# The first SwiGLU products of layers 0 and 1 in two matmuls a block instead of three

## The chip, the cores and the metric

One core of a Trainium2 chip runs the whole program. The time is device microseconds of one execution. The text names the engines as the profile does: PE multiplies, PEld loads its weights, DVE is the vector engine, ACT the scalar engine, POOL the GpSimd engine, SP issues transfers.

## What is computed

Four residual layers on 256 tokens of 1024 channels. Each layer has a token mixer (short gated convolution in layers 0 and 3, neighbourhood attention in layer 1, a long convolution in layer 2) and then a SwiGLU channel mixer. Ahead of each stands an RMS norm, and each adds to the residual. The change concerns the SwiGLU:

```python
def swiglu(h, w13, w2):                       # h: 256 x 1024, normed
    g, u = jnp.split(h @ w13, 2, axis=-1)     # w13: 1024 x 5632
    return (jax.nn.silu(g) * u) @ w2          # w2: 2816 x 1024
```

Layer 1's window attention and layer 2's filters of length 512 do not change. The filters depend on no input token, so the kernel makes them early.

## The kernel before, in words

**Numbers in two parts.** All large products take float32 operands as a rounded part and a remainder, both in float32r: a weight tile `w` becomes `hi` and `lo`, an activation `x` becomes `xh` and `xl`. A product is `hi·xh + hi·xl + lo·xh`. A *block* here is one 128x128 weight tile against 256 tokens, so a block is three products of 256 columns.

**Two forms of a block.** `mm3` (L122) issues three matmuls of 256 columns into one half of a PSUM bank. `mm2` (L129) issues two. `xh` and `xl` lie beside each other in one tile, so the first streams both as 512 columns past `hi` and fills a whole bank (the left half `hi·xh`, the right half `hi·xl`). The second adds `lo·xh`, 256 columns, to the left half. The two halves must be added afterwards. `join` (L136) does this: ACT copies the right half out of PSUM, DVE adds it to the left half.

**The SwiGLU** is `ffn` (L292). The first product has 44 weight columns a layer (22 for g, 22 for u), each of 8 blocks, so 352 blocks. The second has 8 output tiles of 22 blocks each. `HALVES` (L49) says which layers use the two-matmul form in the first product: layers 2 and 3. They run `product2` (L313), which takes one hidden tile `j` (128 channels) at a time: columns g and u of `j`, two whole banks, and then `gated2` (L296). Layers 0 and 1 run the loop at L352: two hidden tiles at a time in the halves of two banks (four columns), and then `gated` (L334). In the trace `pg` and `pu` are the banks of g and u, `R` is the norm's factor, `hid` the result in two parts, which the second product (bank `po`) reads. The second product uses `mm2` in all four layers, so its block `k` needs the two parts of hidden tile `k`.

**Weights.** `wload` (L99) brings each weight column of 512 KB by a transfer on SP's queue (tile `st`, 5 buffers), ACT rounds it to `hi` (L109, 6 buffers) and DVE or POOL subtracts to make `lo` (6 buffers). `POOL_FILTERS` (L48) gives POOL 17% of the `lo` subtractions in layers 0 and 1. In layers 2 and 3 DVE does them all.

**Filters.** While layers 0 and 1 run their SwiGLU, `fill(j)` (L881) adds one step of the filter work of layer 2 after every second pair of hidden tiles (slots of `FILTER_SLOTS`, L41): either a step of 8 PE matmuls (`ff`) with elementwise work on DVE, ACT and POOL, or a step of 14 PE matmuls (`fl`, `fh`) with a reciprocal, two products and two sums on DVE. `product2` calls `fill(j // 2)` after odd `j`, so the number of slots is the same in both forms.

**Order.** Each engine runs its instructions in the order in which they stand in its own stream. A scheduler sets that order when the program is built. `Pipeline` (L269) only says which step of the loop issues which work. PSUM has 8 banks for everything.

Of the kernel before, what the change touches and what calls it, by code (L numbers as in the profile page):

```python
# [45 lines left out]
AHEAD = 6  # L46

POOL_FILTERS = 0.17  # L48
HALVES = (2, 3)  # L49
LOW_DMA_FROM = 5  # L50


# [1 line left out]
def encoder(ctx: ExitStack, tc: tile.TileContext, A: dict, out: bass.AP):  # L54
# [13 lines left out]
    def bank(name):  # L68
        return pp.tile([P, 512], F32, tag="ps", name=name)
# [222 lines left out]
    def ffn(layer, norm, nxt, fill):  # L292
        with tc.tile_pool(name=f"ffn{layer}", bufs=NP_, side="right") as hp:
# [19 lines left out]
            def product2(line):  # L313
                parts = []
                for j in range(FT):
                    ps = [bank(f"pg{layer}_{j}"), bank(f"pu{layer}_{j}")]
                    for i in range(2):
                        w = wload(A["f_w13"][layer, i * FT + j], D, f"w13_{layer}_{i * FT + j}")
                        if j < 2:
                            parts.append((ps[i], w))  # L320
                            if len(parts) == 4:
                                in_group2(parts, norm)
                        else:
                            in_tile2(ps[i], w, norm)
                        line.tick()
                    if j == 1:
                        line.add(line.now + NORM_LAG, norm.stats)
                        line.add(line.now + NORM_LAG + 1, gated2, 0, before)
                        line.add(line.now + NORM_LAG + 1, gated2, 1, ps)
                    elif j:  # L330
                        line.add(line.now, gated2, j, ps)
                    before = ps
# [16 lines left out]
            line = Pipeline()  # L349
            if layer in HALVES:  # L350
                product2(line)
            for j in range(0 if layer in HALVES else NP_):  # L352
                pg, pu = bank(f"pg{layer}_{j}"), bank(f"pu{layer}_{j}")
# [652 lines left out]
```

## Time and profile before

| what | value |
|---|---|
| three runs | 1216.48, 1219.21, 1221.54 us, median 1219.21 |
| the profiled execution | 1219.07 us, span 1217.3 us |
| mean granted PE clock | 0.997 |
| PE busy | 1194.1 us, 98% of the span |
| weight loads (PEld) | 1105.2 us, 91% |
| DVE busy | 948.5 us, 78% |
| ACT busy | 681.9 us, 56% |
| POOL busy | 180.1 us, 15% |

The span runs from the first profiled instruction to the last. 1.8 us of the profiled execution's time lie outside it. Matmuls are pipelined, so a matmul's own duration is longer than the step to the next one. The pace of PE is read from the starts of matmuls. DVE and ACT start an instruction slightly before the one ahead has ended, so their busy time in a window is a little less than the sum of durations.

### The profile page before, as it was taken

What the parts mean: (1) busy time and instruction counts of PE and PEld (TensorE: products, weight loads), DVE (VectorE), ACT (ScalarE), POOL (GpSimd) and SP (SyncE); (2) the same over time, 40 slices, a digit from 0 to 9 for tenths busy, and PEclk for the clock granted to TensorE, in tenths of its full rate; (3) what the DMA queues carried; (4) which work ended last, traced back from release to release, by engine and by line L of the source; (5) the groups of instructions that cost most, each with busy time, mean ns of one, the idle gap of its engine ahead of it and who ended that gap; (6) DMA issues with size and microseconds to landing.
All of it is one profiled execution on the core that took longest, in us unless ns stands there. A gap on an engine that the chain in (4) does not pass through costs nothing.

```text
span 1217.3 us, 21366 instructions
## 1 busy us (share of the span) xinstructions
PE 1194.1 (98%) x8242; PEld 1105.2 (91%) x8242; DVE 948.5 (78%) x1421; ACT 681.9 (56%) x1096; POOL 180.1 (15%) x175
## 2 busy tenths in 40 slices
PE   7999999999998999999999999999999999999998
PEld 5899999988998999999898999888888889888887
DVE  6987877988676678788948996887765888787753
ACT  5655554555567665455547775665554555665531
POOL 0001121331454122232322120000000000000000
PEclk9999999999999999999998999999999999999999
DMA  9754656566666555666689996655565554655661
GB/s 309 233 191 135 215 176 206 171 209 210 218 182 189 164 187 175 198 193 179 208 255 268 296 282 211 208 191 190 175 190 190 194 191 162 210 183 187 175 203 39
DMA packets 72095, 241.82 MB, mean 199 GB/s; under 512 B 10231, under 2 KB 11641, under 8 KB 71865
## 3 DMA queue, kind: packets, MB, share of 16 engines
q1 hardware_dynamic: 61408, 211.68, 54.1%
q0 software_dynamic: 8256, 22.84, 8.1%
q10 hardware_dynamic: 2328, 5.93, 1.3%
q8 instruction: 65, 1.06, 0.4%
q14 instruction: 38, 0.30, 0.1%
HBM read 234.10 MB, written 6.29 MB: 197 GB/s over the span
## 4 chain that ended last, share of the span: by engine, by line
PE 91%; DMA 3%; DVE 2%; POOL 2%; ACT 1%; issue 1%; SPq 0%; POOLq 0%; ACTq 0%; DVEq 0%
PE po L133 14%; PE ai L133 7%; PE po L134 7%; PE pu L133 7%; PE pg L133 7%; PE ai L134 4%; PE pu L125 3%; PE pg L125 3%; PE pu L126 3%; PE pg L127 3%; PE pu L127 3%; PE pg L126 3%; PE pu L134 3%; PE pg L134 3%; PE ci L127 2%; PE ci L125 2%
## 5 line engine op out<-in xcount | busy, mean ns | idle before, releaser
L109 ACT CAST hiw<-stw 128x1024 fp32r<-128x1024 f32 (+1 forms) x276 | 280.3, 1024 | 245.0 <-PE po L133 67.0
L78 DVE TENSOR_TENSOR low<-stw,hiw 128x1024 fp32r<-128x1024 f32 (+1 forms) x254 | 305.6, 1208 | 121.2 <-ACT hiw L109 119.7
L133 PE MATMUL po<-hid,hiw 128*128 128x512 f32 x704 | 248.3, 396 | 0.0
L134 PE MATMUL po<-hid,low 128*128 128x256 f32 x704 | 197.8, 281 | 0.0
L133 PEld LDWEIGHTS po<-hid,hiw 128*128 128x128 f32 x704 | 132.1, 188 | 31.9 <-DVE hid L78 0.5
L133 PE MATMUL ai<-xsm,hiai 128*128 128x512 f32 x376 | 133.7, 398 | 0.0
L134 PEld LDWEIGHTS po<-hid,low 128*128 128x128 f32 x704 | 132.6, 188 | 0.0
L133 PE MATMUL pg<-xsf,hiw 128*128 128x512 f32 x352 | 126.8, 396 | 0.0
L133 PE MATMUL pu<-xsf,hiw 128*128 128x512 f32 x352 | 126.5, 395 | 0.0
L134 PE MATMUL ai<-xsm,loai 128*128 128x256 f32 x376 | 106.0, 282 | 0.0
L125 PE MATMUL pu<-xsf,hiw 128*128 128x256 f32 x352 | 99.3, 282 | 0.0
L125 PE MATMUL pg<-xsf,hiw 128*128 128x256 f32 x352 | 99.0, 281 | 0.0
L126 PE MATMUL pu<-xsf,hiw 128*128 128x256 f32 x352 | 98.9, 281 | 0.0
L127 PE MATMUL pg<-xsf,low 128*128 128x256 f32 x352 | 98.9, 281 | 0.0
L134 PE MATMUL pg<-xsf,low 128*128 128x256 f32 x352 | 98.9, 281 | 0.0
L127 PE MATMUL pu<-xsf,low 128*128 128x256 f32 x352 | 98.9, 281 | 0.0
L126 PE MATMUL pg<-xsf,hiw 128*128 128x256 f32 x352 | 98.9, 281 | 0.0
L134 PE MATMUL pu<-xsf,low 128*128 128x256 f32 x352 | 98.8, 281 | 0.0
L78 POOL TENSOR_TENSOR low<-stw,hiw 128x1024 fp32r<-128x1024 f32 (+1 forms) x22 | 53.9, 2452 | 223.7 <-ACT hiw L109 193.1
L133 PEld LDWEIGHTS ai<-xsm,hiai 128*128 128x128 f32 x376 | 71.0, 189 | 17.1
L133 PEld LDWEIGHTS pu<-xsf,hiw 128*128 128x128 f32 x352 | 66.1, 188 | 15.7
L133 PEld LDWEIGHTS pg<-xsf,hiw 128*128 128x128 f32 x352 | 66.1, 188 | 15.4
(238 smaller groups left out, 3035.7 us busy)
## 6 DMA issues: line engine op xcount, KB each, us to landing
stw<-in_f_w SPq DMA_DIRECT2D x208, 512.0 KB, 3.4
stw<-in_f_w SPq DMA_DIRECT2D x64, 448.0 KB, 3.4
stai<-in_a_w_in SPq DMA_DIRECT2D x45, 512.0 KB, 3.7
stbi<-in_b_w_qkv SPq DMA_DIRECT2D x24, 512.0 KB, 4.2
stci<-in_c_w_in SPq DMA_DIRECT2D x24, 512.0 KB, 9.2
loci<-in_c_w_in POOLq DMA_DIRECT2D x19, 512.0 KB, 14.1
stao<-in_a_w_out SPq DMA_DIRECT2D x16, 512.0 KB, 3.2
hf<-ht POOLq DMA_DIRECT2D x16, 256.0 KB, 3.4
```

Source lines behind the costliest of these rows:

```text
L78: (eng or ve).tensor_tensor(out=out_, in0=a, in1=b, op=op)
L109: ac.copy(out=hi[:, c], in_=st[:, c])
L125: pe.matmul(ps, hi[:, ws], xh, start=first, stop=False, **kw)
L126: pe.matmul(ps, hi[:, ws], xl, start=False, stop=False, **kw)
L127: pe.matmul(ps, lo[:, ws], xh, start=False, stop=last, **kw)
L133: pe.matmul(ps, hi[:, ws], hl.rearrange("p s t -> p (s t)"), start=first, stop=False)
L134: pe.matmul(ps[:, :T], lo[:, ws], hl[:, 0], start=False, stop=last)
```

## The change

One number tuple changes, and with it the form of the first product in layers 0 and 1:

```diff
-HALVES = (2, 3)
+HALVES = range(4)
```

Layers 0 and 1 now run `product2` and `gated2` in place of the loop at L352 and `gated`. Their 704 blocks are issued as two matmuls with two weight loads each, not three and three. g and u of one hidden tile are loaded one after the other. Each hidden tile gets two copies on ACT and two additions on DVE (`join`), and its elementwise steps work on one tile of 256 tokens where they worked on two.

The first place is PE in layer 0, near the end of the first product: the first three contraction steps of the g column of hidden tile 20 (`xsf` is the normed input in two parts, `hiw` and `low` the two parts of the weight). Before:

```order
L125 MATMUL pg_10_2701<-xsf_0_1107,hiw_0_20_2704 128x256
L126 MATMUL pg_10_2701<-xsf_0_1107,hiw_0_20_2704 128x256
L127 MATMUL pg_10_2701<-xsf_0_1107,low_0_20_2705 128x256
L125 MATMUL pg_10_2701<-xsf_2_1118,hiw_0_20_2704 128x256
L126 MATMUL pg_10_2701<-xsf_2_1118,hiw_0_20_2704 128x256
L127 MATMUL pg_10_2701<-xsf_2_1118,low_0_20_2705 128x256
```

and now:

```order
L133 MATMUL pg_20_2578<-xsf_0_1107,hiw_0_20_2581 128x512
L134 MATMUL pg_20_2578<-xsf_0_1107,low_0_20_2582 128x256
L133 MATMUL pg_20_2578<-xsf_2_1118,hiw_0_20_2581 128x512
L134 MATMUL pg_20_2578<-xsf_2_1118,low_0_20_2582 128x256
L133 MATMUL pg_20_2578<-xsf_4_1131,hiw_0_20_2581 128x512
L134 MATMUL pg_20_2578<-xsf_4_1131,low_0_20_2582 128x256
```

Each block has one matmul less and as many columns as before.

The second place is DVE in layer 0, where the first product ends: up to the instruction that writes the last part of the last hidden tile (`hid`). `tg`, `tu` and `s` hold g and u outside PSUM, `c` is the copy of a bank's right half, `Rf` the norm's factor; `rl` and `eo` belong to the filters. Before:

```order
L78 TENSOR_TENSOR hh_9_2739<-sg_9_2736,tu_9_2734 128x512
L78 TENSOR_TENSOR hid_9_2741<-hh_9_2739,hid_9_2741 128x2x256
L78 TENSOR_TENSOR tg_10_2834<-pg_10_2701,Rf_1451 128x512
L78 TENSOR_TENSOR low_0_1_0_2952<-stw_0_1_0_2950,hiw_0_1_0_2951 128x1024
L78 TENSOR_TENSOR low_0_1_8_2974<-stw_0_1_8_2972,hiw_0_1_8_2973 128x896
L78 TENSOR_TENSOR tu_10_2835<-pu_10_2702,Rf_1451 128x512
L706 RECIPROCAL rl_2851<-fl_2845 128x256
L78 TENSOR_TENSOR hh_10_2840<-sg_10_2837,tu_10_2835 128x512
L78 TENSOR_TENSOR eo_2862<-fh_2855,rl_2851 128x512
L78 TENSOR_TENSOR eo_2871<-fh_2864,rl_2851 128x512
L78 TENSOR_TENSOR hid_10_2842<-hh_10_2840,hid_10_2842 128x2x256
```

and now:

```order
L78 TENSOR_TENSOR s_20_2662<-s_20_2662,Rf_1399 128x512
L78 TENSOR_TENSOR low_0_1_8_2842<-stw_0_1_8_2840,hiw_0_1_8_2841 128x896
L78 TENSOR_TENSOR hh_20_2672<-sg_20_2670,s_20_2662 128x256
L78 TENSOR_TENSOR s_21_2699<-pg_21_2638,c_210_2700 128x256
L78 TENSOR_TENSOR low_0_1_15_2862<-stw_0_1_15_2860,hiw_0_1_15_2861 128x896
L78 TENSOR_TENSOR hid_20_2674<-hh_20_2672,hid_20_2674 128x256
L78 TENSOR_TENSOR s_21_2699<-pu_21_2639,c_211_2703 128x256
L78 TENSOR_TENSOR s_21_2699<-s_21_2699,Rf_1399 128x512
L78 TENSOR_TENSOR hh_21_2709<-sg_21_2707,s_21_2699 128x256
L706 RECIPROCAL rl_2719<-fl_2713 128x256
L78 TENSOR_TENSOR hid_20_2674<-hh_21_2709,hid_20_2674 128x256
```

After the last u bank (`pu_21`) DVE now has three more instructions up to `hid`, and the reciprocal stands between `hh` and `hid`. The subtraction for a weight that the second product needs later (`low_0_1_15`) now stands ahead of `hid`.

## Rows read from the trace of the kernel before

**Rows 1.** The page, part 4: shares of the span in the chain that ended last, by engine.

```profile
PE 91%; DMA 3%; DVE 2%; POOL 2%; ACT 1%; issue 1%; SPq 0%; POOLq 0%; ACTq 0%; DVEq 0%
```

**Rows 2.** Windows (us, PE, PEld, DVE, ACT, POOL, PEclk, DMA share, GB/s): first products.

```profile
103.60:235.90 132.30, 132.30 (x1111) 131.33 (x1110) 106.89 (x137) 70.00 (x91) 30.34 (x22) 1.00 0.58 184
425.60:557.30 131.70, 131.70 (x1114) 131.59 (x1114) 104.90 (x125) 69.69 (x88) 33.73 (x25) 1.00 0.60 188
750.60:873.80 123.20, 123.04 (x711) 107.76 (x710) 100.66 (x166) 75.53 (x139) 0.70 (x1) 1.00 0.57 185
```

**Rows 3.** Timeline of PE: start us, us, engine, line, instruction, [idle before].

```profile
166.27 0.29 PE L125 MATMUL pg<-xsf,hiw 128*128 128x256 f32 x1
188.99 0.40 PE L704 MATMUL fl<-lr,onesr 128*128 128x256 f32 x2
574.49 0.40 PE L133 MATMUL po<-hid,hiw 128*128 128x512 f32 x1
590.02 0.28 PE L679 MATMUL ff<-hiw,hd 128*128 128x256 f32 x1
771.06 0.48 PE L133 MATMUL pu<-xsf,hiw 128*128 128x512 f32 x1
873.76 0.39 PE L133 MATMUL po<-hid,hiw 128*128 128x512 f32 x1
1046.35 0.48 PE L133 MATMUL pu<-xsf,hiw 128*128 128x512 f32 x1
1151.02 0.39 PE L133 MATMUL po<-hid,hiw 128*128 128x512 f32 x1
```

**Rows 4.** Groups by form, layer 0, first product. Count, then busy us, mean ns, idle before.

```profile
L78 DVE TENSOR_TENSOR low<-stw,hiw 128x1024 fp32r<-128x1024 f32 x36 | 45.6, 1272 | 18.3 <-ACT hiw L109 17.8 <-POOL lr L78 0.6
L78 POOL TENSOR_TENSOR low<-stw,hiw 128x1024 fp32r<-128x1024 f32 x7 | 17.2, 2463 | 67.4 <-ACT hiw L109 43.8 <-PE pu L127 22.0 <-DVE low L78 1.6
L78 DVE TENSOR_TENSOR hh<-sg,tu 128x512 f32<-128x512 f32 x10 | 10.5, 1048 | 0.3
L78 DVE TENSOR_TENSOR hid<-hh,hid 128x512 fp32r<-128x512 f32 x10 | 9.7, 970 | 2.7 <-ACT hid L144 2.7
L78 DVE TENSOR_TENSOR tg<-pg,Rf 128x512 f32<-128x512 f32 x11 | 7.5, 682 | 1.2 <-PE pg L127 1.2
```

**Rows 5.** Groups by form, layer 2, first product (two-matmul form, no filters).

```profile
L78 DVE TENSOR_TENSOR s<-s,Rf 128x512 f32<-128x512 f32 x21 | 14.5, 690 | 0.5
L78 DVE TENSOR_TENSOR s<-pg,c 128x256 f32<-128x256 f32 x22 | 9.2, 418 | 0.0
L78 DVE TENSOR_TENSOR hh<-sg,s 128x256 f32<-128x256 f32 x21 | 8.8, 418 | 0.5 <-ACT sg L304 0.5
L78 DVE TENSOR_TENSOR hid<-hh,hid 128x256 fp32r<-128x256 f32 x20 | 8.4, 419 | 0.7
```

**Rows 6.** Timeline, layer 0, where the first product ends: PE, then DVE, then POOL.

```profile
234.20 0.40 PE L704 MATMUL fl<-lr,onesr 128*128 128x256 f32 x2
235.87 0.39 PE L133 MATMUL po<-hid,hiw 128*128 128x512 f32 x1
...
227.22 2.60 DVE L78 TENSOR_TENSOR hh<-sg,tu 128x512 f32<-128x512 f32 x1
235.01 1.75 DVE L706 RECIPROCAL rl<-fl 128x256 f32<-128x256 f32 x1
238.41 0.86 DVE L78 TENSOR_TENSOR hid<-hh,hid 128x512 fp32r<-128x512 f32 x1
...
226.78 2.50 POOL L78 TENSOR_TENSOR low<-stw,hiw 128x896 fp32r<-128x896 f32 x1 [2.78 <-ACT hiw L109]
```

**Rows 7.** Timeline of PEld, layer 2, where the first product ends.

```profile
881.50 0.19 PEld L133 LDWEIGHTS po<-hid,hiw 128*128 128x128 f32 x1 [0.27 <-DVE hid L78]
```

**Rows 8.** Busy time in windows: last 22 us of the first product, layers 0, 1.

```profile
213.40:235.40 22.00, 22.00 (x189) 22.00 (x188) 20.82 (x25) 13.31 (x17) 7.47 (x7) 1.00 0.61 179
535.30:557.30 22.00, 22.00 (x188) 22.00 (x188) 15.69 (x20) 9.29 (x11) 4.24 (x4) 1.00 0.67 198
```

## The prediction

> **What bounds the kernel now.** I read the chain that ended last first: PE holds 91% of it [rows 1], so the time is decided by how fast PE gets through its blocks and by what keeps it from starting one. Next the windows of the first products: in layers 0 and 1 PE is busy for the whole window (132.30 of 132.30 us and 131.70 of 131.70), with DVE at 106.89 and 104.90 us and ACT at some 70 [rows 2]. So the change can gain only by a better pace of PE, and it can lose only where PE must wait. Then PE's timeline, for the pace [rows 3]; the groups by form of layer 0 and of layer 2, for what the old and the new elementwise steps cost on DVE [rows 4, 5]; and last the place where a first product ends and the second begins [rows 6 to 8], for there PE first wants what DVE makes.
>
> **PE.** The change removes one matmul and one weight load of each of 704 blocks (two layers, 352 each); the columns, 768 a block, stay. The old form: 64 blocks lie between the starts 166.27 and 188.99, so 22.72 us / 64 = 355.0 ns a block [rows 3]. The new form can be read in three places [rows 3]. In layer 1's second product, with filter steps before and behind, 44 blocks take 15.53 us, 353.0 ns. In layer 3's first product 296 blocks take 104.67 us, 353.6 ns. In layer 2's first product 296 blocks take 102.70 us, 347.0 ns. Why layer 2 is quicker no row tells. I take 353.3, since the second product of layer 1 is the nearest: it too is broken by filter matmuls. That gives 704 x 1.7 ns = **1.2 us less**. The bounds are 1.0 us (353.6) and 5.6 us (347.0).
>
> **DVE through the product.** A pair of hidden tiles now takes two products with `R` (0.68 each), `hh` (1.05) and `hid` (0.97) [rows 4], 3.4 us. In the new form one tile takes two joins (0.42 each), one product with `R` (0.69), `hh` (0.42) and `hid` (0.42) [rows 5], 2.36 us, so 4.73 a pair: 1.34 us more. Eleven pairs make 14.7 us a layer, and DVE goes from 106.9 to about 121.6 of some 131.6 us. ACT gets two copies more a tile; layer 2, which has them and no filters, has ACT at 75.53 of 123.20 [rows 2], so in layers 0 and 1 I expect some 90, with room. I cost both at nothing while the product runs. What hides them is that `low` is made up to six weight columns ahead (a column is 8 blocks, 2.8 us) and that banks of PSUM are left for the next tiles. Without that cover the 14.7 us a layer would meet only what DVE has idle now, 25 us.
>
> **Where the second product begins.** Here the cover ends. The second product wants hidden tile `k` at its block `k`. So PE reaches the last hidden tiles some 20 blocks, 7 us, after the last matmul of the first product (call that T), and whatever DVE is late by then is a wait of PE. Now this is covered: in layer 0 T is 234.20, the filter's 14 matmuls run up to 235.87, block 20 is wanted at 235.87 + 20 x 0.353 = 242.9, and the last `hid` ends at 238.41 + 0.86 = 239.27 [rows 6], 3.7 us early.
>
> Layer 2 shows the new form at that place without filters: T is 873.76 [rows 3], and at 881.50 a weight load of PE starts after 0.27 us of waiting for `hid` [rows 7]. So it is wanted at T + 7.5 and ready at T + 7.7.
>
> In layer 0 it is wanted later by the filter's matmuls, 235.87 - 234.20 = 1.67 us: T + 9.1. It is ready later by three things. The reciprocal, 1.75 us [rows 6], now stands between the last `hh` and the last `hid` (second piece of the order). DVE has a lag: in the last 22 us it is busy for 20.82 [rows 8], and two pairs add 2.7, 23.5 for 22.0, so 1.5 us. And one hold by POOL: an `hh` that took 2.60 us began 0.44 us after a POOL `low` of 2.50 and ended with it to about half a microsecond [rows 6], where an instruction of that form takes 0.69 [rows 5]: 1.9 us. Sum: T + 7.7 + 1.75 + 1.5 + 1.9 = T + 12.9, **3.8 us late**.
>
> The Trainium skill has a rule for that hold ("SBUF — State Buffer", section "Who interferes with whom"): a DVE instruction with two SBUF inputs competes with a GpSimd instruction that reads SBUF, and one with a PSUM input does not. The trace agrees: `tg`, which reads PSUM, has a mean of 682 ns beside POOL's seven subtractions, `hh` one of 1048 [rows 4]. By that rule the change sets one more instruction a tile open to holds (the product of `s` with `R` reads SBUF alone, as `tg` and `tu` did not), which is the third rival below.
>
> In layer 1 the filter step at this place has 8 matmuls of 256 columns, at a third of 355.0 ns 0.95 us, so `hid` is wanted at T + 8.4. Several short filter instructions stand between `hh` and `hid` there; I price them as the reciprocal, since no row has them in that position. DVE has no lag: 15.69 + 2.7 = 18.4 of 22 us [rows 8]. With one hold: T + 7.7 + 1.75 + 1.9 = T + 11.35, **2.9 us late**. The bounds for each layer: no hold and no lag leave 0.3 and 1.0 us; a second hold or a second column's subtraction (1.27 us [rows 4]) ahead of `hid` makes it some 2 us more each, 10.7 in all.
>
> **Sum.** Against the profiled execution, 1219.07 us, which stands at the median of the runs (1219.21): 1219.07 - 1.2 + 3.8 + 2.9 = **1224.6 us**. With the bounds of the wait (1.3 to 10.7) and a pace up to the quicker one, the forecast's own range is 1220 to 1230. The measurement can tell about 0.5% from no change, here 6.1 us: the forecast, 5.4 over, lies just inside.
>
> **Rivals.**
> *The cover suffices.* DVE's lag is absorbed by its idle time and POOL makes no subtraction in those few microseconds. For it: POOL has only 30 us of work in 132 [rows 2], and DVE's order is made anew by the scheduler, so that `hid` may meet no hold. Against it: the slack is 1.4 us in layer 0 even before the reciprocal (9.1 against 7.7). What is left is a wait of 0 to 1.3 us: 1217.9 to 1219.2, say 1218.5. This is the side on which the change is not slower. Chance 0.25.
>
> *The quicker pace.* All 704 blocks run at 347.0 ns as in layer 2. For it: the form is the same. Against it: layers 1 and 3 [rows 3] run it at 353. Without waits that is 1219.07 - 5.6 = 1213.5; with the waits of the forecast 1220.2, which is in the forecast's own range. Chance of the first 0.09.
>
> *DVE becomes the bound.* It decides where `low` no longer comes ahead of PE, that is, when DVE needs more than the 131.6 us. Layer 0 stands at 121.6. Today's holds are 0.36 us for each `hh` and 0.28 for each `hid` over the 0.69 of the unheld form [rows 4, 5], 0.64 a pair and 7.0 us a layer; these are in the old sum, and the new sum has none yet, for layer 2 has no such POOL work. If they fall on the new instructions as they did on the old, DVE is at 128.6; if the product with `R` takes as many again as `hh` did, at 132.6, and PE then waits for `low` and the lag at the end is the whole backlog. For it: the filters come in bursts, and the last 22 us of layer 0 are above the line already. Against it: layer 1 has 2 us less on DVE, and in the idle time of the new form POOL's holds are partly waits that DVE has anyway. Price: about 1 us in the product and a backlog of two columns of subtraction and two more holds at each end, some 6.4 us over the forecast's waits in each layer that it strikes, so 1224.6 + 6.4 = 1231 for one layer and 1237 for both. Chance 0.16.
>
> *That the change does not do what it says* is excluded by the order on PE, where each block has one matmul less.
>
> **The numbers.** The forecast keeps 0.50; its own range, 1220 to 1230, is cut in its middle by the line of 1225.3, so 0.25 is no change and 0.25 slower. The cover that suffices (0.25) is no change, but for 0.03 that I give to faster for the spread of the runs (1216.48 to 1221.54). The quicker pace (0.09) lies 0.46% under the time of now, on the other line: 0.05 faster, 0.04 no change. DVE as the bound (0.16) is slower throughout. Faster 0.05 + 0.03 = 0.08, same 0.25 + 0.22 + 0.04 = 0.51, slower 0.25 + 0.16 = 0.41. The range of 8 in 10 goes from 1214.5 (the cover that suffices, less that spread, and part of the quicker pace) to 1236 (DVE as the bound in nearly both layers).
>
> **What would show it.** Right: in layers 0 and 1 blocks of the first product start 353 ns apart; DVE's busy time there is 118 to 130 us; PE or its weight loads wait 2 to 5 us for `hid` some 20 blocks into the second product; the reciprocal and a longer `hh` or product with `R` stand beside a POOL `low` ahead of that `hid`. Wrong: no such wait (then the cover suffices), 347 ns a block (the quicker pace), or PE waits for `low` inside the first product (DVE is the bound). A wait that falls elsewhere, for a transfer or a bank of PSUM, would be a mechanism that I have not seen.

## The result, and the profile after

The changed kernel takes 1231.28 us (median of 4 runs, 1228.8 to 1231.9), the kernel before 1218.53 us (median of 4 runs, 1216.48 to 1221.54). The ratio is 1.0092, 95% interval 1.0076 to 1.0107: slower, by more than the half per cent that can be told from no change. The profiled execution took 1231.34 us, with a span of 1229.5 us, 12.2 more than before.

First the page of the changed kernel, its parts on the engines and on the chain (before, the chain was 91% PE and 2% DVE [rows 1]):

```profile
PE 1197.2 (97%) x7538; PEld 1073.4 (87%) x7538; DVE 987.4 (80%) x1553; ACT 709.5 (58%) x1228; POOL 185.0 (15%) x175
...
PE 86%; DVE 6%; DMA 3%; POOL 2%; issue 2%; ACT 1%; POOLq 0%; SPq 0%; DVEq 0%; ACTq 0%
```

5% of the chain have gone from PE to others, 4 of them to DVE. The view of PE's waits says where (what waited, for whom, us in total, times, the longest):

```profile
PE po L133 <- DVE hid L78: 7.8, 2, 4.7
...
PE psnf L199 <- POOL rtf L193: 1.3, 3, 0.6
```

The first line was not there before. The second, for the norms, is 0.9 us more than its 0.4 of before. PE's timeline gives the places of the two long waits, and the pace:

```profile
191.35 0.39 PE L133 MATMUL pu<-xsf,hiw 128*128 128x512 f32 x1
213.94 0.28 PE L679 MATMUL ff<-hiw,hd 128*128 128x256 f32 x1
234.67 0.40 PE L704 MATMUL fl<-lr,onesr 128*128 128x256 f32 x2
236.34 0.40 PE L133 MATMUL po<-hid,hiw 128*128 128x512 f32 x1
247.05 0.50 PE L133 MATMUL po<-hid,hiw 128*128 128x512 f32 x1 [3.12 <-DVE hid L78]
255.27 0.28 PE L679 MATMUL ff<-hiw,hd 128*128 128x256 f32 x1
560.32 0.28 PE L679 MATMUL ff<-hiw,hd 128*128 128x256 f32 x1
573.58 0.79 PE L133 MATMUL po<-hid,hiw 128*128 128x512 f32 x1 [4.72 <-DVE hid L78]
574.38 0.63 PE L133 MATMUL po<-hid,hiw 128*128 128x512 f32 x1
575.02 0.63 PE L133 MATMUL po<-hid,hiw 128*128 128x512 f32 x1
583.26 0.40 PE L704 MATMUL fl<-lr,onesr 128*128 128x256 f32 x2
```

The first two rows are 64 blocks of the first product of layer 0: 22.59 us, 353.0 ns a block, where the old form took 355.0 [rows 3]. The wait of layer 0 ends 12.4 us after the last matmul of its first product (234.67), the wait of layer 1 ends 13.3 us after its own (560.32).

The rows at 574.38 and 575.02 show something that the prediction had not. Behind the wait of layer 1 a block takes 640 ns (574.38 to 575.02). The windows ahead of the wait and behind it (us, PE, PEld, DVE, ACT, POOL, PEclk, DMA share, GB/s) give the reason:

```profile
561.30:568.70 7.40, 7.40 (x44) 6.32 (x42) 7.23 (x14) 4.81 (x10) 0.00 (x0) 1.00 0.83 244
...
573.90:576.00 2.10, 2.10 (x7) 1.81 (x7) 2.01 (x5) 2.10 (x4) 0.00 (x0) 0.50 0.53 196
```

The granted clock was 0.50, which is the lower of TensorE's two levels (1.2 GHz), and it had been 1.00 ahead of the wait. So the 88 matmuls (44 blocks) from 561.28 to the next filter step (583.26) took 21.98 us, where 44 blocks without a wait take 15.53 [rows 3]: 4.7 us of waiting and 1.7 of a slow clock. In layer 0 those from 236.34 to 255.27 took 18.93, 3.4 us more, with no slow stretch.

These two places make 9.8 of the 12.2 us. Layer 2's second product, whose code did not change, adds 1.0 by its pace (last section). The changed blocks give back 704 x 2.0 ns = 1.4 us, but the first products as a whole did not get shorter. From their first block to the first block of the second product they take 132.40 and 132.20 us (windows below), and before it was 132.30 and 131.70 [rows 2]. Waits for the norm and other small pieces took back what the pace gave, and 0.6 us more. The rest, 0.8 us, lies elsewhere.

DVE's load came out at the number that was forecast (but see the part on the prediction): the windows of the two first products, which had 106.89 and 104.90 us of it [rows 2], now read

```profile
103.90:236.30 132.40, 131.88 (x758) 114.27 (x757) 120.84 (x191) 79.24 (x147) 32.47 (x21) 1.00 0.57 176
429.10:561.30 132.20, 131.48 (x763) 114.75 (x762) 119.27 (x179) 79.23 (x145) 35.43 (x25) 1.00 0.58 176
```

And the end of layer 0's first product on DVE, then POOL (beside [rows 6]):

```profile
233.51 2.01 DVE L78 TENSOR_TENSOR s<-s,Rf 128x512 f32<-128x512 f32 x1
...
242.94 0.42 DVE L78 TENSOR_TENSOR s<-pu,c 128x256 f32<-128x256 f32 x1
...
244.97 1.75 DVE L706 RECIPROCAL rl<-fl 128x256 f32<-128x256 f32 x1
246.63 0.36 DVE L78 TENSOR_TENSOR hid<-hh,hid 128x256 fp32r<-128x256 f32 x1
...
232.83 2.13 POOL L78 TENSOR_TENSOR low<-stw,hiw 128x896 fp32r<-128x896 f32 x1 [4.17 <-ACT hiw L109]
```

The last bank of u is full near 234.9, and DVE reads it only at 242.94. So the lateness is there before the last tile's own chain begins. The product with `R` at 233.51 took 2.01 us beside POOL's subtraction, where the form takes 0.69 [rows 5]. In layer 1 such a meeting comes earlier (DVE, then POOL):

```profile
552.37 3.77 DVE L78 TENSOR_TENSOR low<-stw,hiw 128x1024 fp32r<-128x1024 f32 x1
...
552.63 2.40 POOL L78 TENSOR_TENSOR low<-stw,hiw 128x1024 fp32r<-128x1024 f32 x1
```

Here it is one of DVE's own subtractions that takes 3.77 us for some 1.22. And there is a second meeting right ahead of the last `hid` of layer 1, with a subtraction that POOL began at 570.19 (2.18 us) and a filter instruction behind it:

```profile
570.75 1.91 DVE L78 TENSOR_TENSOR sd<-fr 128x256 f32<-128x256 f32 x1
572.58 0.94 DVE L78 TENSOR_TENSOR hid<-hh,hid 128x256 fp32r<-128x256 f32 x1
```

In e7, a later run without POOL's subtractions, these two take 0.43 us each (at 563.37 and 563.90). So 2.5 and 2.0 us of layer 1's lateness can be read one by one as holds.

### The profile page after: what moved, and what is told of

It is laid out like the page before. It is cut to its first block, busy times and chain, and to the rows that moved or that the text cites. A ratio compares the mean times of both kernels' runs of the same rounds, so it can differ in the third digit from the quotient of the medians.

```text
span 1229.5 us, 20310 instructions
## 1 busy us (share of the span) xinstructions
PE 1197.2 (97%) x7538; PEld 1073.4 (87%) x7538; DVE 987.4 (80%) x1553; ACT 709.5 (58%) x1228; POOL 185.0 (15%) x175
## 4 chain that ended last, share of the span: by engine, by line
PE 86%; DVE 6%; DMA 3%; POOL 2%; issue 2%; ACT 1%; POOLq 0%; SPq 0%; DVEq 0%; ACTq 0%
PE po L133 13%; PE pu L133 12%; PE pg L133 12%; PE ai L133 7%; PE po L134 6%; PE pu L134 6%; PE pg L134 6%; PE ai L134 4%; DVE low L78 2%; PE ci L127 2%; PE ci L125 2%; PE ci L126 2%; PE accao L127 1%; PE accao L125 1%; PE accao L126 1%
## 5 line engine op out<-in xcount | busy, mean ns | idle before, releaser
L133 PE MATMUL pu<-xsf,hiw 128*128 128x512 f32 x704 | 254.5, 397 | 0.1
L133 PE MATMUL pg<-xsf,hiw 128*128 128x512 f32 x704 | 254.5, 397 | 0.0
L133 PEld LDWEIGHTS pu<-xsf,hiw 128*128 128x128 f32 x704 | 132.2, 188 | 32.4 <-issue 0.3
L133 PEld LDWEIGHTS pg<-xsf,hiw 128*128 128x128 f32 x704 | 132.1, 188 | 31.6
L134 PEld LDWEIGHTS pu<-xsf,low 128*128 128x128 f32 x704 | 132.7, 189 | 0.0
L134 PEld LDWEIGHTS pg<-xsf,low 128*128 128x128 f32 x704 | 132.7, 189 | 0.0
L304 ACT ACTIVATE sg<-s 128x256 f32<-128x256 f32 x88 | 36.8, 418 | 65.8 <-DVE s L78 64.7
L109 ACT CAST hiai<-stai 128x1024 fp32r<-128x1024 f32 (+1 forms) x49 | 48.8, 1013 | 40.1 <-PE ai L133 23.0
L134 PEld LDWEIGHTS ai<-xsm,loai 128*128 128x128 f32 x376 | 71.5, 190 | 0.1
L78 DVE TENSOR_TENSOR loai<-stai,hiai 128x1024 fp32r<-128x1024 f32 (+1 forms) x49 | 57.1, 1177 | 17.3 <-ACT hiai L109 16.8
```

The costliest lines, as they stand in the source:

```text
L78: (eng or ve).tensor_tensor(out=out_, in0=a, in1=b, op=op)
L109: ac.copy(out=hi[:, c], in_=st[:, c])
L133: pe.matmul(ps, hi[:, ws], hl.rearrange("p s t -> p (s t)"), start=first, stop=False)
L134: pe.matmul(ps[:, :T], lo[:, ws], hl[:, 0], start=False, stop=last)
L304: ac.activation(sg, s[:, :T], AF.Silu)
```

## The experiments

Two theories were to be told apart. **The load**: DVE has 14 us more to do in each first product and is late whoever does the rest. **The holds**: DVE could do its work in time, but POOL's `low` subtractions make it late. And for both it was to be shown that the wait for `hid` is what the time goes into.

### One layer alone

```diff
-HALVES = (2, 3)
+HALVES = (0, 2, 3)     # e1; (1, 2, 3) in e2
```

> Only layer 0 takes the two-matmul form. Theory (DVE is late with the last hidden tiles, and PE waits for them at the start of that layer's second product): a wait for hid of about 3.4 us in layer 0 and none in layer 1, in all 2 to 5 us over before. Rival (the loss is not in these waits but in the pace and the phases of PE elsewhere, such as layer 2's second product, which took 1.0 us more): no fixed share for layer 0, the wait may be there but the time does not follow it.

> Only layer 1 takes the two-matmul form. Theory: a wait for hid of about 6.4 us in layer 1 and none in layer 0, in all 5 to 8 us over before; with the run of layer 0 alone the two add up to the 11 to 12 us of the whole change. Rival (one layer's loss is brought on by the other, through weights or DVE work that is carried over): the sum of the two runs differs from the whole by more than 3 us.

Layer 0 alone: 1.0036 (1.0021 to 1.0051), 4.4 us, with one wait for `hid` of 3.4 us. Layer 1 alone: 1.0061 (1.0037 to 1.0086), 7.4 us, with one of 4.7 us. Together 11.8 us, where the whole change has 11.2 by its ratio. So each layer brings its own loss, and the waits mark it. In e1 the clock fell behind the wait of 3.4 us too, as it had not in the changed kernel's layer 0 (window of 2.5 us behind it):

```profile
247.50:250.00 2.50, 2.50 (x9) 2.11 (x9) 2.50 (x4) 0.94 (x1) 0.56 (x1) 0.50 0.00 0
```

### The second product in another order

Output tile 1's first 15 blocks come ahead of output tile 0's last 7 (e3: with the change; e4: in the kernel before).

```diff
             for m in range(KT):
...
+                if m == 0:
+                    todo = [(0, 0), (0, 1), (1, 0), (1, 1), (0, 2)]
+                elif m == 1:
+                    todo = [(1, 2)]
+                else:
+                    todo = [(m, 0), (m, 1), (m, 2)]
```

> The change, with the last 7 blocks of output tile 0 of the second product put behind the first 15 of output tile 1, in all layers: hidden tiles 15 to 21 are wanted 15 blocks, 5.3 us, later. Theory (PE only waits because block 20 comes before its hidden tile): the wait of 3.4 us in layer 0 goes, that of 6.4 in layer 1 falls to about 1 us, in all 8 to 9 us under the changed kernel, near 1222. Rival (DVE is the bound, and a wait that is avoided here comes back as a wait for low or for hid a few blocks later): under 3 us gained.

> The same order of the second product in the kernel before. Theory: no wait for hid stood there to be removed (0.27 us in layer 2 alone), so within 3 us of before, 1216 to 1221. Rival (the new order is better or worse by itself, through PSUM banks or the order of weights): more than 3 us off, and then e3 is to be read against this run.

e4: 0.9994 (0.9982 to 1.0006), nothing, as expected. e3: 1.0075 (1.0049 to 1.0102), 1228.79 us, so some 2 us won, not 8 to 9. The rival was nearer. The waits for `hid` are gone but for 0.3 us, and others stand in their place (e3's waits of PE from 300 to 640 us):

```profile
PE pqt L529 <- DVE qn L78: 6.4, 1, 6.4
PE fl L719 <- POOL lr L78: 3.5, 1, 3.5
```

The second line is in layer 1's second product: the filter's step, which hangs on DVE and POOL as `hid` does, was late as well. So DVE's lateness was not cured by asking for one tile later. The first line is in layer 1's mixer, in code that the edit does not touch; what brought it there was not settled.

### POOL's share

```diff
-POOL_FILTERS = 0.17
+POOL_FILTERS = 0.0     # e5; 0.34 in e6
```

> The change with no low subtraction on POOL: DVE gets some 8 more of 1.25 us a layer (10 us), and loses the holds by them. In the changed kernel the means over the unheld 690 and 418 ns give holds of 8 to 9 us a layer on the elementwise steps. Theory of the holds (POOL's reads make DVE late): the waits for hid fall to 0 to 2 us in all. Theory of the load (DVE has too much to do whoever does it): DVE's busy time stays at about 120 us a layer and the waits stay within 3 us of the 9.8 in all, or grow.

> The change with POOL's share of the subtractions doubled, 0.34: DVE gives up some 8 more of 1.25 us a layer. Theory of the holds: the elementwise steps lose 8 us more a layer, DVE's busy time stays near 120 us, and the waits for hid grow or stay near 10 us. Theory of the load: DVE's busy time falls to about 111 us a layer and the waits fall under 4 us in all.

e5: 1.0007 (0.9992 to 1.0023). The whole loss is gone, though DVE has all the subtractions to do. No wait for `hid` is left; one of 1.9 us for a bank of PSUM in layer 1 has come (`pu` waits for `s`). The steps take their unheld time. e5, layer 1, DVE by form:

```profile
L78 DVE TENSOR_TENSOR s<-s,Rf 128x512 f32<-128x512 f32 x21 | 14.4, 684 | 0.1
...
L78 DVE TENSOR_TENSOR hid<-hh,hid 128x256 fp32r<-128x256 f32 x20 | 8.2, 409 | 0.0
```

In the changed kernel's layer 1 these two had means of 791 and 572 ns. DVE's busy time hardly moved (windows of e5's two first products):

```profile
104.60:236.30 131.70, 131.55 (x759) 114.11 (x757) 117.93 (x205) 82.89 (x152) 11.76 (x13) 1.00 0.59 183
426.00:561.10 135.10, 133.04 (x763) 116.06 (x762) 116.42 (x193) 83.38 (x150) 13.74 (x17) 0.99 0.58 184
```

118 and 116 us against 121 and 119. So busy time was not the measure: much of what POOL "took over" came back as held time on DVE.

e6: 1.0273 (1.0251 to 1.0295), 33 us slower than before. DVE had some 8 subtractions fewer a layer, yet its busy time rose (windows of the two first products, now 7 to 9 us longer than in the changed kernel):

```profile
105.20:244.30 139.10, 134.69 (x759) 116.38 (x757) 123.89 (x181) 78.34 (x147) 46.58 (x28) 0.98 0.53 164
442.60:583.90 141.30, 133.29 (x762) 115.86 (x761) 122.14 (x170) 78.58 (x143) 51.64 (x32) 0.99 0.51 165
```

and PE waited inside the first product too, as in the prediction's third rival (e6, layer 1):

```profile
PE pu L133 <- DVE s L78: 3.6, 2, 2.0
...
PE pu L134 <- DVE low L78: 1.9, 1, 1.9
```

The load theory expected the waits to fall here, and to stay in e5. It falls on both.

### POOL's share by transfer

ACT writes the negative of the weight's rounded part, and a transfer adds the weight to it; DVE's work is that of the changed kernel.

```diff
+            if pool and not isinstance(src, list):
+                ac.activation(lo[:, c], st[:, c], AF.Copy, scale=-1.0)
+                gp.dma_start(out=lo[:, c], in_=src[:, c], accum_op=ALU.add)
+                continue
             tt(lo[:, c], st[:, c], hi[:, c].bitcast(F32), ALU.subtract, gp if pool else ve)
```

> The change with POOL's share of the low subtractions made by ACT and an accumulating transfer, as layer 2's mixer does: DVE's own work is the same, no POOL subtraction reads beside it, ACT has 8 more copies of 1 us a layer. Theory of the holds: elementwise means fall to 690 and 418 ns, DVE to about 112 us a layer, the waits for hid to 0 to 2 us, in all near 1221. Theory of the load (DVE's own instructions alone fill it): the waits stay above 6 us. It could also turn into a wait for the transfer, which took 14 us in layer 2.

1.0028 (1.0014 to 1.0042), 1223.25 us. No wait of PE for `hid` is left, and DVE's busy time has fallen to 112.82 and 111.73 us, as the theory of the holds expects (e7's windows of the two first products):

```profile
104.20:238.60 134.40, 131.87 (x759) 114.24 (x758) 112.82 (x200) 91.03 (x164) 17.64 (x22) 1.00 0.71 206
428.30:559.70 131.40, 131.26 (x762) 114.68 (x762) 111.73 (x188) 89.86 (x161) 22.85 (x25) 1.00 0.74 216
```

So some 8 us of the 120.84 and 119.27 in the changed kernel are held time. The last possibility in the text above has come true too (e7, waits of PE in layer 0):

```profile
PE pg L138 <- DMA low<-in_f_w: 2.5, 1, 2.5
```

### The filter step moved

```diff
-FILTER_SLOTS = (range(0, 19, 2), range(2, 17, 2))
+FILTER_SLOTS = ((0, 2, 4, 6, 8, 11, 12, 14, 16, 18), (2, 4, 6, 8, 11, 12, 14, 16))
```

> The change with the filter step at the end of the first product moved behind output tile 0 of the second product, in layers 0 and 1: the reciprocal (layer 0) and the short filter instructions (layer 1) no longer stand ahead of the last hid, but PE has no 14 or 8 filter matmuls to do before the second product either. Theory (the filter's instructions are 1.75 us of the lateness, the rest is DVE's lag): the waits become 3.4 - 1.75 + 1.67 = 3.3 us in layer 0 and about 6 us in layer 1, so no change within 3 us. Rival (the filter step's instructions make most of the lateness): the waits fall under 3 us in all.

1.0113 (1.009 to 1.0135), beside 1.0092 for the change itself; the waits for `hid` are 8.6 us in all, four of them. With the filter step gone from there, PE gets the last `hid` at T + 12.5 in layer 0 and T + 12.3 in layer 1, where it was T + 12.4 and T + 13.3 (T is, as in the prediction, the end of the first product's matmuls). So these instructions are not most of what makes it late. But in layer 0 DVE now makes two subtractions where the reciprocal stood, so this run does not price the reciprocal by itself. Both expectations missed the other effect: the step now stands inside the second product and waits there itself (`fl` 1.2 us for POOL's `lr`).

### The control, and POOL off at the end alone

e9 is the kernel before with `POOL_FILTERS = 0.0`. e10 is the changed kernel, with POOL's share set to 0 from hidden tile 16 to output tile 1, in layers 0 and 1:

```diff
                     before = ps
+                    if j == 15:
+                        held, share[0] = share[0], 0
+                return held
...
+                if m == 2:
+                    share[0] = held
```

> The kernel before with no low subtraction on POOL, as the control of e5. Theory (in the old form the last hidden tile is 3.7 us early, so POOL's holds cost PE nothing and taking them away gives nothing): within 2 us of before, so that the change without POOL's subtractions (e5, 1220.3) neither wins nor loses against it. Rival (POOL's subtractions cost before several us too): 1212 to 1216, and then the two-matmul form loses even without the holds.

> The change with no low subtraction on POOL from hidden tile 16 up to output tile 1 of the second product, in layers 0 and 1, and its share as before elsewhere. It takes some 3 subtractions a layer from POOL and gives DVE 3.7 us more to do there. Theory (the holds near the end decide, since DVE's lag drains over the last tiles where nothing holds it): the waits for hid fall to 0 to 2 us in all, near 1221. Rival (holds over the whole product build the lag): the waits stay over 5 us.

e9: 0.9991 (0.9981 to 1.0001). The old form neither wins nor loses without POOL's subtractions: it has the slack. e10: 1.0002 (0.9993 to 1.0012), 1220.07 us: three subtractions taken from POOL in layer 0 and four in layer 1 undo the whole loss. No wait of PE for `hid` is left, though DVE is busier in the first product than in the changed kernel:

```profile
103.80:236.20 132.40, 131.87 (x758) 114.29 (x757) 122.35 (x200) 82.15 (x153) 26.03 (x19) 1.00 0.57 182
```

The end of layer 0's first product in e10, PE and then DVE:

```profile
234.57 0.40 PE L709 MATMUL fl<-lr,onesr 128*128 128x256 f32 x2
...
237.34 0.41 DVE L78 TENSOR_TENSOR s<-pu,c 128x256 f32<-128x256 f32 x1
...
239.94 1.75 DVE L711 RECIPROCAL rl<-fl 128x256 f32<-128x256 f32 x1
241.61 0.35 DVE L78 TENSOR_TENSOR hid<-hh,hid 128x256 fp32r<-128x256 f32 x1
```

The last bank of u is read 2.8 us after PE's last matmul of the product, not 8.3, and `hid` is ready at T + 7.4 (241.96 - 234.57), not T + 12.3. The order of the last three instructions, the reciprocal among them, is the same. In layer 1 it is T + 7.0, not T + 13.2:

```profile
556.07 0.28 PE L684 MATMUL ff<-hiw,hd 128*128 128x256 f32 x1
...
562.66 0.40 DVE L78 TENSOR_TENSOR hid<-hh,hid 128x256 fp32r<-128x256 f32 x1
```

In e10 two things change at once: without these subtractions on POOL the scheduler also orders DVE anew. In layer 0 the product with `R` of the last tile but three starts at T - 5.4 in the changed kernel and at T - 5.5 in e10, so the 4.9 us arise behind it. There the changed kernel has one subtraction more and three idle gaps of 0.61, 0.44 and 0.54 us, beside one long hold of 1.3 us (2.01 for 0.69). So e10's 4.9 us are not holds alone.

e7 separates the two. In layer 0 its DVE runs the same instructions in the same order as the changed kernel's from 218.94 (221.26 there) up to the last `hid`, with the reciprocal and the three gaps where they were. Only POOL's subtractions are missing (e7, PE and then DVE):

```profile
236.91 0.40 PE L708 MATMUL fl<-lr,onesr 128*128 128x256 f32 x2
...
231.37 0.69 DVE L78 TENSOR_TENSOR s<-s,Rf 128x512 f32<-128x512 f32 x1
...
243.19 0.36 DVE L78 TENSOR_TENSOR hid<-hh,hid 128x256 fp32r<-128x256 f32 x1
```

`hid` is ready at T + 6.6 here (243.55 - 236.91), and at T + 12.3 in the changed kernel. The row at 231.37 is the counterpart of the one at 233.51 there: it starts at T - 5.5, and there at T - 1.2. So of the 5.7 us 1.3 are the hold that is seen, and 4.4 are lag that DVE had carried to this place (ahead of 218.94 the order differs in places). In layer 1 `hid` is ready at T + 5.6 in e7, and at T + 13.2 in the changed kernel; there the order is not the same throughout.

### PE's pace

e11 turns the two matmuls of every second block, on e5: 512, 256, 256, 512 columns. e12 joins this with POOL's share 0 in layer 0 and e10's edit in layer 1.

```diff
+        two = lambda s: pe.matmul(ps, hi[:, ws], hl.rearrange("p s t -> p (s t)"), start=first, stop=s)
+        one = lambda s: pe.matmul(ps[:, :T], lo[:, ws], hl[:, 0], start=False, stop=s)
+        for i, f in enumerate((one, two) if swap else (two, one)):
+            f(last and i == 1)
```

> The kernel of e5 with the order of a block's two matmuls turned in every second block: 512, 256, 256, 512 columns. It measures PE's pace alone, which ran at 347.0 and at 353.3 ns a block in the same program. Theory (the pace is a phase that PE falls into after a wait and does not hang on the order): 346 to 354 ns a block, within 3 us of e5. Rival (the slow pace comes from the alternation of long and short): all blocks of SwiGLU at 347 or less, 2112 of them by 6 ns, some 12 us under e5.

> The change with three things joined: no low subtraction on POOL in layer 0 (its first product took 130.2 us so in e5, against 130.8 before), POOL off at the end of the first product in layer 1 (e10), and the turned order of e11 (351.5 ns a block wherever the other order ran at 353.3, but also where it ran at 347.0). Theory (with the waits gone PE's pace is what is left, some 2 us in all): 1216 to 1219 where before gives 1220, no wait for hid and none for a bank of PSUM. Rival (what PE gains in blocks is lost in the next wait for a norm, a filter or a mixer): 1219 to 1222, the same as before.

e11: 1.0007 (0.9996 to 1.0018). 64 blocks of layer 0 (e11, PE):

```profile
166.33 0.40 PE L131 MATMUL pu<-xsf,hiw 128*128 128x512 f32 x1
...
188.82 0.40 PE L704 MATMUL fl<-lr,onesr 128*128 128x256 f32 x2
```

22.49 us, 351.4 ns a block: 1.6 ns better than 353.0, but the stretch of layer 2 that ran at 347.0 takes 351.7 (104.09 us for 296 blocks). The rival, 347 or less everywhere, is out. e12: 0.9993 (0.9984 to 1.0003), 1219.12 us, all waits for `hid` and for PSUM gone. That is no gain that can be told from nothing. No version here beats the kernel before.

## Why the prediction was right, and where it was not

**The mechanism held, its sizes did not.** PE waits for the last `hid` at the start of the second product in both layers. This costs 3.4 and 6.4 us, where 3.8 and 2.9 were forecast. The time, 1231.28 us, lies in the range (1214.5 to 1236), 6.7 us above the forecast of 1224.6, and on the side of "slower", which had 0.41 against 0.51 for "same". The likeliest verdict was thus the wrong one.

**PE's pace**: 2.0 ns a block, where 1.7 was taken. Right, and the row chosen (layer 1's second product) was the right one. But the gain was taken as a gain in time, and the first products did not get shorter.

**DVE's load**: 121.6 us were forecast for layer 0, 120.84 came. That is luck. e7, with the same work on DVE and no POOL subtraction, has 112.82: 6 us over the old 106.89, where 14.7 were added. Part of the difference is that the prediction added durations, although DVE starts an instruction slightly before the one ahead has ended. The other 8 us of the 120.84 are held time, which the forecast's sum did not have. The step "I cost both at nothing while the product runs" held: PE waited for no `low`.

**"DVE has no lag" in layer 1 failed.** It was read from DVE's busy time in 22 us of the old kernel plus the new work, 18.4 of 22. But a lag is carried, and POOL makes it: DVE met POOL's subtraction at 552.37 (2.5 us) and had not caught up when the product ended. `hid` came at T + 13.2, not T + 11.35. The one hold that was priced there, 1.9, came (2.0, at 570.75 and 572.58).

**The sums came near by errors that cancel.** The forecast had `hid` at T + 9.45 without lag and hold, from layer 2's 7.7 and 1.75 for the reciprocal. In e7, where the reciprocal stands at its place in layer 0, it comes at T + 6.6 in layer 0 and T + 5.6 in layer 1. So the base was 2.9 and 3.9 us too long. And lag and holds are 5.7 and 7.6 us, by the difference to the changed kernel, where 3.4 and 1.9 were priced. In layer 0 the two errors leave T + 12.3 for T + 12.9, in layer 1 they leave 1.9 us too little.

**The clock was not priced.** A wait of 4.7 us brought 1.7 more at the lower level.

**The rivals.** "The cover suffices" was wrong here, but it is what e10 does: a few subtractions decide it. "DVE becomes the bound" gave 1231 for one layer, which is the time that came, but not by its mechanism: its holds on the new instructions came, but DVE was not full and PE waited for no `low`. e6 is the kernel in which that mechanism is seen.

**The rule on DVE and GpSimd** (the Trainium skill, "SBUF — State Buffer", section "Who interferes with whom") is borne out on the point that the prediction drew from it. The product with `R`, newly open to holds, had a mean of 848 ns in layer 0 (690 unheld [rows 5]), while the joins, which read PSUM, stayed at 415. Without POOL's subtractions it was 684.

## What to carry to other kernels

An offload to another engine has to be priced by what it does to the busy time of the engine that it relieves: here a doubled offload made the relieved engine busier, and taking seven subtractions back at the right place was worth the whole loss. When a change moves work onto an engine that is in order, follow its lateness from tile to tile up to the place where it is wanted, since busy time in a window shows neither lag nor holds. And take a wait of PE of some microseconds as more than its own length, for the clock can be at its lower level behind it.

## What the runs showed of the hardware that was not expected

**The clock behind a wait.** After 4.7 us of waiting (changed kernel, layer 1) PE ran at a granted clock of 0.50 for 3.3 us, 640 ns a block. In e2 the same wait of 4.7 us brought 5.3 us of it, and in e1 one of 3.4 us brought 5.8. After 1.9 us in e5 (the wait for a bank, layer 1) the clock fell too (0.56 from 492 to 494 us), and after 3.1 us in the changed kernel's layer 0 it did not. So the length of the wait alone does not settle it.

**Two paces of the same code.** The same 296 blocks of layer 2's first product ran at 347.0 ns a block in the kernel before, in the changed one and in most runs, and at 353.6 in e4, e8 and e10; its second product has both paces as well. Before, and in the changed kernel (the ends of 176 blocks from 873.76 [rows 3] and from the second row here), then e10's 296 blocks:

```profile
934.99 0.39 PE L133 MATMUL ai<-xsm,hiai 128*128 128x512 f32 x1
```

```profile
884.75 0.39 PE L133 MATMUL po<-hid,hiw 128*128 128x512 f32 x1
...
946.99 0.40 PE L133 MATMUL ai<-xsm,hiai 128*128 128x512 f32 x1
```

```profile
770.45 0.48 PE L133 MATMUL pu<-xsf,hiw 128*128 128x512 f32 x1
...
875.12 0.39 PE L133 MATMUL po<-hid,hiw 128*128 128x512 f32 x1
```

61.23 us against 62.24 for the second product, and 104.67 us for the first, which is 102.70 in the kernel before [rows 3]. In layers 2 and 3 of these runs the pace changes only where PE or its weight loads have waited (for a norm or for `hid`) and then stays for the stretch. What decides it was not found; in e11's order layers 0 and 2 had one pace, 351.4 and 351.7.
